# A 31-tap depthwise convolution: from POOL and diagonal matrices to 128x32 matrices over shifted copies

## The chip, the core and the metric

The kernel runs on one core of one Trainium2 chip. The metric is the device time of one execution in microseconds; the times are medians of several runs. Engines are named as the profile names them: PE (TensorE), DVE (VectorE), ACT (ScalarE), POOL (GpSimd) and SP (SyncE, which issues the DMAs).

## The reference, cut to what matters

The whole model is a chain of blocks over 256 positions of 1024 channels: attention with a chunked recurrent mixer, cross-attention, a feed-forward block, this convolution module, a sparse attention and more feed-forward blocks. The change lies in the convolution module alone:

```
def conformer_conv_module(h, w_in, b_in, w_dw, b_dw, ln_g, ln_b, w_out):
    a, g = jnp.split(h @ w_in + b_in, 2, axis=-1)
    u = a * jax.nn.sigmoid(g)
    u = lax.conv_general_dilated(
        u, w_dw[:, None, :].astype(u.dtype), window_strides=(1,),
        padding=[(CONV_WIDTH - 1, 0)], dimension_numbers=('NWC', 'WIO', 'NWC'),
        feature_group_count=D_MODEL) + b_dw
    uf = u.astype(jnp.float32)
    mu = jnp.mean(uf, axis=-1, keepdims=True)
    var = jnp.mean(jnp.square(uf - mu), axis=-1, keepdims=True)
    uf = (uf - mu) * lax.rsqrt(var + LN_EPS) * ln_g.astype(jnp.float32) + ln_b.astype(jnp.float32)
    u = jax.nn.silu(uf).astype(h.dtype)
    return u @ w_out
```

CONV_WIDTH is 31: each channel is convolved over time with its own 31 taps, causally. The input `h` is the normalised residual.

## The kernel before

Channels lie on the 128 partitions, in eight tiles (m = 0 to 7), time (256) along the free axis. For each tile `conformer` (L930) makes the two halves of the input product, the gated tile `cu`, the 31 taps, and its share of the sums for the layer norm; at the end all tiles are normalised and the output product (`proj("c_out")`, PE lines L215 to L217) follows.

The input product of tiles 0 to 2 is a split one (three fast passes, L215 to L217, 48 matmuls a tile), that of tiles 3 to 7 takes the weights as they were loaded, in fp32 (L990, 32 matmul rows, for tiles 3 and up). DVE multiplies it by the broadcast reciprocal root `bc_x` (L971, L973: `cag`), ACT applies tanh and bias (L975, L976), DVE forms `cu` (L977).

The taps of a tile are dealt out to three engines by two tables. PE takes CONV_PE taps (45 in all): ACT builds a diagonal matrix `cdg` for each (L1042) and PE multiplies `cu` by it into the bank `bt` (L1048). POOL takes CONV_GP taps (78): ACT makes the product `cpr` (L1028; the first of a tile L1025), POOL adds it to `cyp` (L1029). DVE takes the rest with fused multiply-adds on `cy` (L1011, L1013 the first, L1015 the others). DVE then adds the bank (L1057), POOL or DVE adds `cyp` (L1059), for tiles 0 to 2 a mean is subtracted (L1071, POOL), ACT squares (L338) and PE adds up the sums (L1077). Behind the last tile come mean, variance and root on DVE (L1091 and on), two broadcasts by PE (L327), the normalising on DVE and ACT and the split into `yy`. The residual is rescaled on DVE (L438), eight operations, by a second root `rs_g` that POOL computes (L303 to L312).

The order around the change is written out by hand: `CONF_AT` gives each step a due time and a spacing, and `timed()` steps generators by it; `need()` holds one until its input is there. A scheduler then orders the instructions per engine. SP issues only weight loads in this stretch: a raw tile is loaded (L181), ACT casts it (L198), DVE or POOL subtracts the cast (L200) for the split products.

Of the kernel before, what the change touches and what calls it, by code (L numbers as in the profile page):

```python
# [103 lines left out]
class Net:  # L104
# [825 lines left out]
    def conformer(self, first, pool):  # L930
        nc = self.nc
        W = 31
        us = [pool.tile([P, S], F32, name=f"cu{m}") for m in range(KT)]
# [3 lines left out]
        rb = zb = cb = None  # L937
        bt, yp = [None] * KT, [None] * KT
        have = set()

        def need(*keys):
            while not have.issuperset(keys):
                yield

        def tap(m, t):

            return wh[:, m * W + W - 1 - t : m * W + W - t]


        wh = pool.tile([P, KT * W], F32, name="cwh")  # L950
        o = POFF["c_w"][0]
        nc.gpsimd.tensor_scalar(wh, self.par[:, o : o + KT * W], 0.5, None, op0=ALU.mult)
        bh = pool.tile([P, KT], F32, name="cbh")
        o = POFF["c_bin"][0] + KT
        nc.gpsimd.tensor_scalar(bh, self.par[:, o : o + KT], 0.5, None, op0=ALU.mult)

        for m in range(KT):
            nc.vector.tensor_scalar(xg[:, m, :], self.x[:, m, :], gg[:, m : m + 1], None, op0=ALU.mult)

        def inp(m):  # L960
            nonlocal rb, zb
            b = b0
            if m:
                b, pb = product_of(m)
            yield
# [12 lines left out]
            have.add(f"u{m}")

        def product_of(m):  # L980
            nonlocal rb, zb
            w = self.chunk("c_in", m, **({"stop": "c_out"} if m < KT - 1 else {"room": 2}))
            pb = self.bank()
            b = [pb[:, 0:S], pb[:, S : 2 * S]]
            raw = [r.rearrange("p (k c) -> p k c", k=4) for r in w] if m >= CONV_N3 else None

            def product(i, k):
                c = slice(i * P, i * P + P)
                if raw:
                    nc.tensor.matmul(b[i][:, 0:S], raw[k // 4][:, k % 4, c], xg[:, k, :],  # L990
                                     start=(k == 0), stop=(k == KT - 1))
                else:
                    self.mm3(b[i][:, 0:S], w[k][:, :, c], self.xx[:, k], k == 0, k == KT - 1)

            for i in range(2):
                for k in range(KT):
                    product(i, k)
                if m == 1 and i == 0:
                    rb = self.bcast(r12, "x")
                    zb = self.zbank(2 * NT)  # L1000
            return b, pb
# [3 lines left out]
        def dv(m):  # L1005
            yield from need(f"u{m}")
            y, u = ys[m], us[m]
            if m > 2:
                yield from need("c")
                nc.scalar.activation(y, cb, AF.Identity, bias=self.col("c_b", m), scale=-1.0)  # L1010
                nc.vector.scalar_tensor_tensor(y, u, tap(m, 0), y, op0=ALU.mult, op1=ALU.add)  # L1011
            else:
                nc.vector.tensor_scalar(y, u, tap(m, 0), self.col("c_b", m), op0=ALU.mult, op1=ALU.add)  # L1013
            for t in range(1 + CONV_PE[m], W - CONV_GP[m]):
                nc.vector.scalar_tensor_tensor(y[:, t:S], u[:, 0 : S - t], tap(m, t), y[:, t:S], op0=ALU.mult, op1=ALU.add)  # L1015
                if t % 4 == 0:
                    yield
            have.add(f"d{m}")
            yield

        def gp(m):
            yield from need(f"u{m}")
            u, t0 = us[m], W - CONV_GP[m]
            y = yp[m] = pool.tile([P, S], F32, name="cyp", tag="cyp", bufs=4)
            nc.scalar.mul(y[:, t0:S], u[:, 0 : S - t0], tap(m, t0))  # L1025
            for t in range(t0 + 1, W):
                pr = pool.tile([P, S], F32, name="cpr", tag="cpr", bufs=4)
                nc.scalar.mul(pr[:, t:S], u[:, 0 : S - t], tap(m, t))  # L1028
                nc.gpsimd.tensor_tensor(y[:, t:S], y[:, t:S], pr[:, t:S], op=ALU.add)  # L1029
                if t % 4 == 0:  # L1030
                    yield
            have.add(f"g{m}")
            yield

        def pe(m):
            yield from need(f"u{m}")
            n = CONV_PE[m]
            for c in range(0, n, 4):
                dg = []
                for t in range(c + 1, min(c + 4, n) + 1):  # L1040
                    d = pool.tile([P, P], F32, name="cdg", tag="cdg", bufs=24)
                    nc.scalar.mul(d, self.ident, tap(m, t))  # L1042
                    dg.append(d)
                yield
                if c == 0:
                    bt[m] = self.bank("bt")
                for t, d in enumerate(dg, c + 1):
                    nc.tensor.matmul(bt[m][:, t:S], d, us[m][:, 0 : S - t], start=(t == 1), stop=(t == n))  # L1048
            have.add(f"p{m}")
            yield  # L1050

        def fin(m):
            nonlocal cb
            yield from need(f"d{m}", f"p{m}")
            y, t0 = ys[m], W - CONV_GP[m]
            if CONV_PE[m]:
                nc.vector.tensor_tensor(y[:, 1:S], bt[m][:, 1:S], y[:, 1:S], op=ALU.add)  # L1057
            yield from need(f"g{m}")
            (nc.gpsimd if m < KT - 2 else nc.vector).tensor_tensor(y[:, t0:S], yp[m][:, t0:S], y[:, t0:S], op=ALU.add)  # L1059
# [19 lines left out]
            have.add(f"s{m}")  # L1079
            yield  # L1080

        def rescale():
            yield from rest

        kinds = {"in": inp, "gp": gp, "dv": dv, "pe": pe, "fin": fin, "x": rescale}
# [556 lines left out]
```

## Time and profile before

| | us |
|---|---|
| median of three runs | 1132.01 (1129.48 to 1132.69) |
| the profiled execution | 1132.2 |
| span of its trace | 1130.4 |
| stage of the change in it: last residual sums to first output matmul | 440.5 to 566.2 |
| mean granted clock of PE over the span | 0.974 of full |

The profile is one execution. The table of stretches gives busy time per engine with the number of instructions and the clock granted to PE; the timeline gives in order of time the start, the length, the engine, the line and operation, the number of instructions run together in the row and, in brackets, the idle time of the engine ahead of it and what ended it. In both kernels the instructions of all other stages stand in the same order on each engine.

### The profile page before, as it was taken

The numbers are of one execution on the slowest core, as the hardware profiler recorded it, in microseconds if no ns is written. First come the engines' busy times: TensorE is split into PE (matmuls) and PEld (weight loads), VectorE is DVE, ScalarE is ACT, GpSimd is POOL, SyncE is SP. The second block draws the span as 40 slices with busy tenths as digits, with TensorE's granted clock in tenths as the row PEclk, the third lists the DMA queues.
The fourth block names the chain that finished last, engine by engine and source line by source line (L and its number), as shares of the span: only waits on it lengthen the run. The fifth ranks groups of instructions, "written<-read, shape, count | busy, mean of one in ns | idle before, by whom it ended". The sixth has DMA issues, their size and how long they took to land.

```text
span 1130.4 us, 19501 instructions
## 1 busy us (share of the span) xinstructions
PE 1070.3 (95%) x7282; PEld 984.6 (87%) x7282; DVE 827.4 (73%) x1654; ACT 638.2 (56%) x1231; POOL 195.4 (17%) x388
## 2 busy tenths in 40 slices
PE   6999999999999999697499999999999999999998
PEld 5899999999999889586398888889998898888887
DVE  5876667768888755999758777765568747777763
ACT  5675556556666544565366666544366746666531
POOL 5120003020000002677512000011332103000000
PEclk9999999999999999888599999999999999999999
DMA  7654444445555752222235565656235024555670
GB/s 233 220 167 158 127 147 155 128 135 191 187 193 178 219 169 71 65 85 93 75 113 176 190 191 183 223 173 189 95 112 189 18 76 149 188 190 192 179 208 31
DMA packets 52439, 171.38 MB, mean 152 GB/s; under 512 B 8440, under 2 KB 10360, under 8 KB 52344
## 3 DMA queue, kind: packets, MB, share of 16 engines
q1 hardware_dynamic: 52344, 170.14, 47.4%
q8 instruction: 57, 0.93, 0.3%
q14 instruction: 38, 0.31, 0.1%
HBM read 169.07 MB, written 1.05 MB: 150 GB/s over the span
## 4 chain that ended last, share of the span: by engine, by line
PE 79%; DVE 12%; ACT 3%; issue 2%; DMA 2%; POOL 1%; SPq 0%; POOLq 0%; ACTq 0%; DVEq 0%
PE pb L223 28%; PE pb L224 14%; PE pb L215 9%; PE pb L216 9%; PE pb L217 9%; DVE cy L1015 5%; DMA wraw<-in_w_in_dram 1%; ACT wpr L198 1%; DVE wpr L200 1%; DVE xx L278 1%; DVE xres L438 1%; DVE xres L395 1%; PE bh L1254 1%; DMA wraw<-in_n_out_dram 1%; PE zb L376 1%
## 5 line engine op out<-in xcount | busy, mean ns | idle before, releaser
L200 DVE TENSOR_TENSOR wpr<-wraw,wpr 128x1024 fp32r<-128x1024 f32 (+1 forms) x298 | 361.1, 1214 | 178.7 <-ACT wpr L198 176.4
L198 ACT CAST wpr<-wraw 128x1024 fp32r<-128x1024 f32 (+1 forms) x304 | 313.4, 1033 | 203.1 <-PE pb L224 96.0
L223 PE MATMUL pb<-xx,wpr 128*128 128x512 f32 x840 | 294.3, 393 | 0.0
L224 PE MATMUL pb<-xx,wpr 128*128 128x256 f32 x840 | 235.5, 280 | 0.0
L223 PEld LDWEIGHTS pb<-xx,wpr 128*128 128x128 f32 x840 | 158.5, 189 | 34.0
L223 PE MATMUL pb<-fhs,wpr 128*128 128x512 f32 x528 | 186.0, 394 | 0.0
L224 PEld LDWEIGHTS pb<-xx,wpr 128*128 128x128 f32 x840 | 158.5, 189 | 0.0
L224 PE MATMUL pb<-fhs,wpr 128*128 128x256 f32 x528 | 147.3, 279 | 0.0
L215 PE MATMUL pb<-xx,wpr 128*128 128x256 f32 x456 | 129.7, 287 | 7.7 <-ACT xx L277 7.7
L216 PE MATMUL pb<-xx,wpr 128*128 128x256 f32 x456 | 130.4, 287 | 2.5 <-DVE xx L278 2.5
L217 PE MATMUL pb<-xx,wpr 128*128 128x256 f32 x456 | 128.9, 283 | 0.0
L223 PEld LDWEIGHTS pb<-fhs,wpr 128*128 128x128 f32 x528 | 99.0, 187 | 23.0
L224 PEld LDWEIGHTS pb<-fhs,wpr 128*128 128x128 f32 x528 | 99.0, 188 | 0.0
L215 PEld LDWEIGHTS pb<-xx,wpr 128*128 128x128 f32 x456 | 86.7, 192 | 9.4 <-ACT xx L277 8.0
L216 PEld LDWEIGHTS pb<-xx,wpr 128*128 128x128 f32 x456 | 87.3, 191 | 4.2 <-DVE xx L278 3.3
L217 PEld LDWEIGHTS pb<-xx,wpr 128*128 128x128 f32 x456 | 87.4, 192 | 0.0
L215 PE MATMUL pb<-yy,wpr 128*128 128x256 f32 x256 | 73.1, 288 | 2.3 <-ACT yy L282 2.3
L216 PE MATMUL pb<-yy,wpr 128*128 128x256 f32 x256 | 72.7, 284 | 0.0
L217 PE MATMUL pb<-yy,wpr 128*128 128x256 f32 x256 | 72.6, 284 | 0.0
L1015 DVE SCALAR_TENSOR_TENSOR cy<-cu,cwh,cy 128x238 f32<-128x238 f32 (+18 forms) x117 | 71.6, 669 | 0.1
L869 ACT COPY ft<-pb 128x256 f32<-128x256 f32 x105 | 38.5, 368 | 55.2 <-PE pb L224 55.2
L1029 POOL TENSOR_TENSOR cyp<-cyp,cpr 128x229 f32<-128x229 f32 (+11 forms) x70 | 59.9, 860 | 26.1 <-ACT cpr L1028 22.0
(428 smaller groups left out, 2077.9 us busy)
## 6 DMA issues: line engine op xcount, KB each, us to landing
wraw<-in_up_dram SPq DMA_DIRECT2D x44, 512.0 KB, 4.0
wraw<-in_up2a_dram SPq DMA_DIRECT2D x44, 512.0 KB, 4.4
wraw<-in_up2b_dram SPq DMA_DIRECT2D x44, 512.0 KB, 3.8
wraw<-in_w_in_dram SPq DMA_DIRECT2D x22, 512.0 KB, 4.6
wraw<-in_n_in_dram SPq DMA_DIRECT2D x20, 512.0 KB, 4.1
wraw<-in_wkv_dram SPq DMA_DIRECT2D x16, 512.0 KB, 3.7
wraw<-in_dn_dram SPq DMA_DIRECT2D x16, 512.0 KB, 4.4
wraw<-in_c_in_dram SPq DMA_DIRECT2D x16, 512.0 KB, 4.1
```

Of the source, the lines that this page charges most:

```text
L198: self.nc.scalar.copy(hi, raws[j])
L200: lane.tensor_tensor(lo, raws[j], hi.bitcast(F32), op=ALU.subtract)
L215: mm(out, left[:, 0], right[:, 0], start=start, stop=False, skip_group_check=True)
L216: mm(out, left[:, 0], right[:, 1], start=False, stop=False, skip_group_check=True)
L217: mm(out, left[:, 1], right[:, 0], start=False, stop=stop, skip_group_check=True)
L223: mm(out, left[:, 0], right, start=start, stop=False, skip_group_check=True)
L224: mm(out[:, 0], left[:, 1], right[:, 0], start=False, stop=stop, skip_group_check=True)
L278: nc.vector.scalar_tensor_tensor(lo, src, g, hi.bitcast(F32), op0=ALU.mult, op1=ALU.subtract)
L376: self.nc.tensor.matmul(zb[:, tt : tt + 1], src[:, tt * P : tt * P + P], self.ones, start=(src is acc), stop=(src is sq))
L869: nc.scalar.copy(t, b[:, 1])
L1015: nc.vector.scalar_tensor_tensor(y[:, t:S], u[:, 0 : S - t], tap(m, t), y[:, t:S], op0=ALU.mult, op1=ALU.add)
L1029: nc.gpsimd.tensor_tensor(y[:, t:S], y[:, t:S], pr[:, t:S], op=ALU.add)
```

## The change

Nothing of the convolution runs on POOL any more, apart from clearing a margin, scaling a bias and the root `rs_g`. PE takes the first 4 x CONV_G[m] taps of tile m (12 for tiles 0 to 5, 16 and 24 for the last two), DVE the others (19, 15 and 7), 112 and 136 in all. The gated tiles now lie in one array `cuz` with 27 zeros ahead of each. `turn(m)` writes a tile to a DRAM buffer `cz` and reads it back into `crp` in another arrangement: partition 32j + c of block i holds channel 32i + c shifted by j, so one matrix of 128 rows and 32 columns sums four taps of 32 channels. Four such matmuls, one for each 32 channels, write four column ranges of 32 in the bank `bt` (a group); a tile has CONV_G groups. The matrices `cwd` come ready from DRAM (new input array `c_dw`, 1.8 MB, eight loads).

The due-time table is gone; a plain loop issues, for each m, the product and gate of tile m + 1, its turn, then the matmul taps, DVE taps and sums of tile m. The scaled input `cxg` is made by ACT instead of DVE, the means of tiles 0 to 2 are subtracted by DVE instead of POOL, and the second part of all output weights' conversion runs on DVE instead of POOL for six of the eight loads.

```diff
-CONV_PE = [4, 1, 1, 4, 1, 15, 11, 8]
-CONV_GP = [8, 10, 10, 10, 14, 6, 9, 11]
+CONV_G = [3, 3, 3, 3, 3, 3, 4, 6]
...
-        lane = self.nc.gpsimd if name == "c_out" and idx > 0 else self.nc.vector
-        lane.tensor_tensor(lo, raws[j], hi.bitcast(F32), op=ALU.subtract)
+        self.nc.vector.tensor_tensor(lo, raws[j], hi.bitcast(F32), op=ALU.subtract)
...
-        us = [pool.tile([P, S], F32, name=f"cu{m}") for m in range(KT)]
+        PAD = 4 * max(CONV_G) - 4
+        ZW = PAD + 3 + S
+        uz = pool.tile([P, KT, ZW], F32, name="cuz")
+        nc.gpsimd.memset(uz[:, :, 0 : PAD + 3], 0.0)
+        us = [uz[:, m, PAD + 3 :] for m in range(KT)]
+        dram = self.ctx.enter_context(self.tc.tile_pool(name="dram", bufs=1, space=bass.MemoryType.DRAM))
+        zs = [dram.tile([32, 4 * ZW], F32, name=f"cz{i}")[:, :] for i in range(4)]
...
+        wd = [pool.tile([P, n, P], F32, name=f"cwd{m}") for m, n in enumerate(CONV_G)]
+        for m, n in enumerate(CONV_G):
+            nc.sync.dma_start(wd[m], self.T["c_dw"][:, m, 0:n, :])
+        reps = [pool.tile([P, 4, ZW], F32, name=f"crp{i}") for i in range(3)]
...
+        def turn(m):
+            z = zs[m % 4]
+            nc.sync.dma_start(bass.AP(tensor=z.tensor, offset=0, ap=[[ZW, 4], [4 * ZW, 32], [1, ZW]]), uz[:, m, :])
+            nc.sync.dma_start(reps[m % 3].rearrange("p j x -> p (j x)")[:, 0 : 4 * ZW - 3],
+                              bass.AP(tensor=z.tensor, offset=0, ap=[[1, 4], [4 * ZW, 32], [1, 4 * ZW - 3]]))
+
+        def pe(m):
+            bt[m] = self.bank("bt")
+            n = CONV_G[m]
+            for i in range(n):
+                for j in range(4):
+                    c = slice(32 * j, 32 * j + 32)
+                    nc.tensor.matmul(bt[m][c, 0:S], wd[m][:, i, c], reps[m % 3][:, j, PAD - 4 * i : PAD - 4 * i + S],
+                                     start=(i == 0), stop=(i == n - 1))
...
-        timed([(u[0], u[1], kinds[u[2]](*u[3:])) for u in CONF_AT])
+        gated(0, None)
+        turn(0)
+        next(rest)
+        for m in range(KT):
+            if m + 1 < KT:
+                gated(m + 1, product(m + 1))
+                turn(m + 1)
+            if m == 0:
+                for k in range(KT):
+                    nc.scalar.mul(xg[:, k, :], self.x[:, k, :], gg[:, k : k + 1])
+            pe(m)
+            dv(m)
+            fin(m)
```

The order of the instructions at three places follows, first in the kernel before, then in the changed one; the lines of the changed kernel are lower by 14 ahead of the stage (L215 is L201 there, L327 is L313).

PE at the start of the stage, before: the broadcast of `rs_n` stands between matmuls of the product of tile 1 (`pb` from `wpr`), which has begun long before it.

```order
L216 MATMUL pb_5180<-xx_75,wpr_5043 128x256
L217 MATMUL pb_5180<-xx_75,wpr_5043 128x256
L215 MATMUL pb_5180<-xx_75,wpr_5043 128x256
L327 MATMUL bcb_5205<-ident_69,rs_n_5133 128x128 [waits DVE_49,PE_49]
L327 MATMUL bcb_5205<-ident_69,rs_n_5133 128x128
L216 MATMUL pb_5180<-xx_75,wpr_5043 128x256
L217 MATMUL pb_5180<-xx_75,wpr_5043 128x256
L215 MATMUL pb_5180<-xx_75,wpr_5043 128x256
L216 MATMUL pb_5180<-xx_75,wpr_5043 128x256
```

The same place after: both broadcasts, of `rs_n` and of POOL's `rs_g`, stand ahead of the product of tile 1.

```order
L202 MATMUL pb_4499<-xx_75,wfi_4571 128x256
L203 MATMUL pb_4499<-xx_75,wfi_4571 128x256
L313 MATMUL bcb_5189<-ident_69,rs_n_5133 128x128 [waits DVE_49,PE_49]
L313 MATMUL bcb_5189<-ident_69,rs_n_5133 128x128
L313 MATMUL bcb_5219<-ident_69,rs_g_5204 128x128 [waits PE_49,Pool_49]
L313 MATMUL bcb_5219<-ident_69,rs_g_5204 128x128
L201 MATMUL pb_5224<-xx_75,wpr_4976 128x256 [waits PE_49]
L202 MATMUL pb_5224<-xx_75,wpr_4976 128x256
L203 MATMUL pb_5224<-xx_75,wpr_4976 128x256
```

The broadcast of `rs_g`, which stood behind the input products of all tiles before, has moved ahead of that of tile 1.

SP, before: only loads of weights, each waiting for the matmuls or conversions that free its buffer.

```order
L181 DMA wraw_5534<-in_c_in_dram 128x1024 [waits DMAHW2_49,PE_49]
L181 DMA wraw_5536<-in_c_in_dram 128x1024 [waits DMAHW3_49,PE_49]
L181 DMA wraw_5561<-in_c_in_dram 128x1024 [waits DMAHW4_49,PE_49]
L181 DMA wraw_5563<-in_c_in_dram 128x1024 [waits DMAHW5_49,PE_49]
L181 DMA wraw_5725<-in_c_out_dram 128x1024 [waits DMAHW6_49,PE_49]
L181 DMA wraw_5727<-in_c_out_dram 128x1024 [waits DMAHW7_49,PE_49]
L181 DMA wraw_5732<-in_c_out_dram 128x1024 [waits DMAHW2_49,DVE_49]
```

SP after, from the turn of tile 3 (write `cz`, read `crp`) to the turn of tile 5; the read waits for the write of its own tile:

```order
L976 DMA cz3_5158<-cuz_5151 4x32x279 [waits DVE_49]
L977 DMA crp0_5184<-cz3_5158 128x1x1113 [waits DMAHW5_49,DMAHW4_49]
L168 DMA wraw_5570<-in_c_in_dram 128x1024 [waits PE_49]
L168 DMA wraw_5572<-in_c_in_dram 128x1024 [waits DMAHW7_49,PE_49]
L976 DMA cz0_5155<-cuz_5151 4x32x279 [waits DVE_49]
L977 DMA crp1_5185<-cz0_5155 128x1x1113 [waits DMAHW1_49,DMAHW0_49]
L168 DMA wraw_5638<-in_c_in_dram 128x1024 [waits DMAHW2_49,PE_49]
L168 DMA wraw_5640<-in_c_in_dram 128x1024 [waits DMAHW3_49,PE_49]
L976 DMA cz1_5156<-cuz_5151 4x32x279 [waits DVE_49]
L977 DMA crp2_5186<-cz1_5156 128x1x1113 [waits DMAHW5_49,DMAHW4_49]
```

Each pair of loads now stands behind a read that waits for a write, and each turn behind the loads of the pair ahead.

PE in the middle of the loop, before: products of two tiles follow each other, then the taps that stand ready.

```order
L990 MATMUL pb_5538<-cxg_5167,wraw_5480 128x256 x4
L990 MATMUL pb_5538<-cxg_5167,wraw_5482 128x256 x4
L990 MATMUL pb_5565<-cxg_5167,wraw_5534 128x256 [waits DMAHW6_49,PE_49]
L990 MATMUL pb_5565<-cxg_5167,wraw_5534 128x256 x3
L990 MATMUL pb_5565<-cxg_5167,wraw_5536 128x256 [waits DMAHW7_49]
L990 MATMUL pb_5565<-cxg_5167,wraw_5536 128x256 x3
L990 MATMUL pb_5565<-cxg_5167,wraw_5534 128x256 x4
L990 MATMUL pb_5565<-cxg_5167,wraw_5536 128x256 x4
L1048 MATMUL bt_5634<-cu3_5154,cdg_5604 128x255
L1048 MATMUL bt_5634<-cu3_5154,cdg_5606 128x254
L1048 MATMUL bt_5634<-cu3_5154,cdg_5608 128x253
```

PE after: the end of the product of tile 4 (`pb_5506`) with sums of tile 2 in it, the taps of tile 3 (`crp0`), the product of tile 5.

```order
L954 MATMUL pb_5506<-cxg_5167,wraw_5051 128x256
L1016 MATMUL zb_5194<-ones_71,sq_5496 128x1 [waits Activation_49]
L1016 MATMUL zb_5194<-ones_71,cy2_5161 128x1
L1016 MATMUL zb_5194<-ones_71,sq_5496 128x1
L954 MATMUL pb_5506<-cxg_5167,wraw_5056 128x256 x4
L986 MATMUL bt_5530<-crp0_5184,cwd3_5171 32x256 [waits DMAHW5_49,PE_49]
L986 MATMUL bt_5530<-crp0_5184,cwd3_5171 32x256 x11
L954 MATMUL pb_5574<-cxg_5167,wraw_5502 128x256 [waits DMAHW2_49,PE_49]
L954 MATMUL pb_5574<-cxg_5167,wraw_5502 128x256 x3
L954 MATMUL pb_5574<-cxg_5167,wraw_5504 128x256 [waits DMAHW3_49]
L954 MATMUL pb_5574<-cxg_5167,wraw_5504 128x256 x3
```

The product of tile m + 2 now always stands behind the matmul taps of tile m, which wait for a DMA.

## Rows read from the trace of the kernel before

**Rows 1.** PE's timeline. Columns: start us, length us, engine, line, operation, count, [idle <- releaser].

```profile
440.52 0.51 PE L415 MATMUL zb<-g,sq 128*128 128x2 f32 x4
...
481.64 0.74 PE L292 MATMUL zb<-ones,cy 128*128 128x1 f32 x4 [4.03 <-DVE zb L287]
...
483.65 16.49 PE L990 MATMUL pb<-cxg,wraw 128*128 128x256 f32 x64
...
499.98 2.30 PE L1048 MATMUL bt<-cu,cdg 128*128 128x255 f32 x10
...
503.82 7.15 PE L990 MATMUL pb<-cxg,wraw 128*128 128x256 f32 x32
...
556.06 0.59 PE L1077 MATMUL zb<-ones,cy 128*128 128x1 f32 x2 [2.52 <-DVE cy L1059]
...
566.16 0.58 PE L215 MATMUL pb<-yy,wpr 128*128 128x256 f32 x1 [2.34 <-ACT yy L282]
```

**Rows 2.** DVE's timeline, same columns.

```profile
441.06 0.16 DVE L320 TENSOR_SCALAR rv<-zb 128x2 f32<-128x2 f32 x1 [0.77 <-PE zb L415]
...
448.64 0.42 DVE L977 SCALAR_TENSOR_TENSOR cu<-cag 128x256 f32<-128x256 f32 x1 [0.34 <-ACT cag L975]
...
452.72 4.92 DVE L1015 SCALAR_TENSOR_TENSOR cy<-cu,cwh,cy 128x249 f32<-128x249 f32 x6
...
527.47 6.53 DVE L1015 SCALAR_TENSOR_TENSOR cy<-cu,cwh,cy 128x236 f32<-128x236 f32 x17
...
543.32 11.85 DVE L438 SCALAR_TENSOR_TENSOR xres<-xres,par,bc_x 128x256 f32<-128x256 f32 x8 [3.05 <-ACT bc_x L330]
...
555.60 0.40 DVE L1059 TENSOR_TENSOR cy<-cyp,cy 128x236 f32<-128x236 f32 x1
```

**Rows 3.** The page's head.

```profile
span 1130.4 us, 19501 instructions
```

**Rows 4.** Table of stretches; the first row names the columns.

```profile
core 0: us, PE busy (x) PEld busy (x) DVE busy (x) ACT busy (x) POOL busy (x), PEclk, DMA share, GB/s
...
441.00:453.00 12.00, 11.47 (x94) 11.25 (x94) 9.54 (x34) 9.29 (x28) 6.51 (x19) 1.00 0.00 0
...
474.00:532.00 58.00, 49.45 (x227) 42.85 (x225) 57.43 (x96) 32.46 (x79) 42.23 (x47) 0.89 0.31 100
...
532.00:556.00 24.00, 9.11 (x32) 8.14 (x32) 18.16 (x23) 9.90 (x20) 21.39 (x18) 0.57 0.25 77
...
441.00:566.00 125.00, 88.62 (x425) 77.88 (x424) 112.29 (x216) 67.99 (x167) 83.57 (x99) 0.80 0.22 72
```

**Rows 5.** Chain of waits through the stage, shares by line.

```profile
by line: DVE cy L1015 47.0%; issue 10.6%; DVE xres L438 8.0%; ACT cdg L1042 4.3%; DVE cu L977 3.1%; DVE cag L973 2.9%; ACT wpr L198 2.3%; DVE cy L1011 2.1%; ACT cpr L1028 2.0%; POOL cyp L1029 2.0%; PE bcb L327 2.0%; DVE cy L1098 1.7%; PE zb
```

**Rows 6.** Costliest groups: the page's for DVE, POOL's from 441 to 591 us.

```profile
L200 DVE TENSOR_TENSOR wpr<-wraw,wpr 128x1024 fp32r<-128x1024 f32 (+1 forms) x298 | 361.1, 1214 | 178.7 <-ACT wpr L198 176.4
...
L200 POOL TENSOR_TENSOR wpr<-wraw,wpr 128x1024 fp32r<-128x1024 f32 x6 | 14.8, 2471 | 18.3 <-ACT wpr L198 18.3
```

**Rows 7.** PE's timeline, two row tiles of 64, in a later stage.

```profile
817.94 0.70 PE L1352 MATMUL bs<-nkT,nqT 64*128 64x256 f32 x4
818.48 0.39 PE L1355 MATMUL bs<-nkT,nqT 64*128 64x128 f32 x4
```

**Rows 8.** DMA queue (packets, MB, share) and issues (count, KB each, us to landing).

```profile
q1 hardware_dynamic: 52344, 170.14, 47.4%
...
wraw<-in_wq_dram SPq DMA_DIRECT2D x8, 512.0 KB, 3.5
...
wraw<-in_dn2a_dram SPq DMA_DIRECT2D x8, 384.0 KB, 3.1
...
gw<-in_gate_w_dram SPq DMA_DIRECT2D x2, 16.0 KB, 5.0
```

**Rows 9.** POOL's timeline.

```profile
446.01 0.20 POOL L312 TENSOR_TENSOR rs_g<-rs_g,rt_g 128x2 f32<-128x2 f32 x1
```

**Rows 10.** Table of stretches, columns as in rows 4.

```profile
481.90:488.70 6.80, 6.55 (x19) 5.46 (x20) 6.24 (x11) 5.85 (x17) 6.29 (x9) 0.50 0.00 0
```

More of the change, by code (lines that the diff above doesn't have):

```diff
@@ L45 @@
     (4.681, 1, "v", 2), (4.986, 1, "v", 3), (5.392, 0.56, "out")]
-CONF_AT = [
[10 rows of a table removed]
-    (19.392, 0.476, "fin", 7)]
 NSA_AT = [
@@ L936, in conformer @@
         b0, (r12, rest, gg) = first
[L937 to L943, printed above, removed]
-        def tap(m, t):
[L947 to L965, printed above, removed]
+        bt, cb = [None] * KT, None
+        def tap(m, t):
+            return self.col("c_w", m * W + W - 1 - t)
@@ new lines, in conformer @@
+        wd = [pool.tile([P, n, P], F32, name=f"cwd{m}") for m, n in enumerate(CONV_G)]
+        for m, n in enumerate(CONV_G):
+            nc.sync.dma_start(wd[m], self.T["c_dw"][:, m, 0:n, :])
+        reps = [pool.tile([P, 4, ZW], F32, name=f"crp{i}") for i in range(3)]
+        bh = pool.tile([P, 2 * KT], F32, name="cbh")
+        o = POFF["c_bin"][0]
+        nc.gpsimd.tensor_scalar(bh, self.par[:, o : o + 2 * KT], 0.5, None, op0=ALU.mult)
+        rb = self.bcast(r12, "x")
+        zb = self.zbank(2 * NT)
@@ new lines, in product @@
+        def product(m):
+            w = self.chunk("c_in", m, **({"stop": "c_out"} if m < KT - 1 else {"room": 2}))
+            pb = self.bank()
+            raw = [r.rearrange("p (k c) -> p k c", k=4) for r in w] if m >= CONV_N3 else None
+            for i in range(2):
+                b, c = pb[:, i * S : i * S + S], slice(i * P, i * P + P)
+                for k in range(KT):
+                    if raw:
+                        nc.tensor.matmul(b, raw[k // 4][:, k % 4, c], xg[:, k, :], start=(k == 0), stop=(k == KT - 1))
+                    else:
+                        self.mm3(b, w[k][:, :, c], self.xx[:, k], k == 0, k == KT - 1)
+            return pb
@@ L966, in inp, with gated @@
+        def gated(m, pb):
             ag = pool.tile([P, 2, S], F32, name="cag", tag="cag", bufs=2)
             if m == 0:
-                while rb is None:
-                    yield
                 for i in range(2):
-                    nc.vector.tensor_tensor(ag[:, i, :], b[i][:, 0:S], rb, op=ALU.mult)
+                    nc.vector.tensor_tensor(ag[:, i, :], b0[i][:, 0:S], rb, op=ALU.mult)
             else:
@@ L977, in inp @@
             nc.vector.scalar_tensor_tensor(us[m], ag[:, 1, :], 1.0, ag[:, 0, :], op0=ALU.add, op1=ALU.mult)
[L978 to L1001, printed above, removed]
+        def turn(m):
[3 more added lines that the diff above has]
+                              bass.AP(tensor=z.tensor, offset=0, ap=[[1, 4], [4 * ZW, 32], [1, 4 * ZW - 3]]))
@@ L1005, in dv @@
+        def pe(m):
[6 more added lines that the diff above has]
+                                     start=(i == 0), stop=(i == n - 1))
         def dv(m):
-            yield from need(f"u{m}")
             y, u = ys[m], us[m]
+            t0 = 4 * CONV_G[m]
@@ L1008, in dv @@
             if m > 2:
-                yield from need("c")
                 nc.scalar.activation(y, cb, AF.Identity, bias=self.col("c_b", m), scale=-1.0)
-                nc.vector.scalar_tensor_tensor(y, u, tap(m, 0), y, op0=ALU.mult, op1=ALU.add)
             else:
-                nc.vector.tensor_scalar(y, u, tap(m, 0), self.col("c_b", m), op0=ALU.mult, op1=ALU.add)
-            for t in range(1 + CONV_PE[m], W - CONV_GP[m]):
+                nc.scalar.activation(y, u, AF.Identity, bias=self.col("c_b", m), scale=0.0)
@@ L1015, in dv @@
+            for t in range(t0, W):
                 nc.vector.scalar_tensor_tensor(y[:, t:S], u[:, 0 : S - t], tap(m, t), y[:, t:S], op0=ALU.mult, op1=ALU.add)
[L1016 to L1050, printed above, removed]
@@ L1052, in fin @@
         def fin(m):
             nonlocal cb
[L1054 to L1059, printed above, removed]
+            y = ys[m]
+            nc.vector.tensor_tensor(y, bt[m][:, 0:S], y, op=ALU.add)
@@ L1065, in fin @@
                 nc.vector.tensor_scalar(c0, z0[:, 0:NT], 1.0 / P, None, op0=ALU.mult)
-                yield
                 cb = self.bcast(c0, "mu", pool)
-                have.add("c")
             if m <= 2:
-                yield from need("c")
-                nc.gpsimd.tensor_tensor(y, y, cb, op=ALU.subtract)
-            yield
+                nc.vector.tensor_tensor(y, y, cb, op=ALU.subtract)
             sq = self.square(y)
-            yield
             for tt in range(NT):
@@ L1078, in fin @@
                                      start=False, stop=(m == KT - 1), skip_group_check=True)
[L1079 to L1085, printed above, removed]
-        timed([(u[0], u[1], kinds[u[2]](*u[3:])) for u in CONF_AT])
+        gated(0, None)
[6 more added lines that the diff above has]
+            if m == 0:
+                for k in range(KT):
+                    nc.scalar.mul(xg[:, k, :], self.x[:, k, :], gg[:, k : k + 1])
+            pe(m)
+            dv(m)
+            fin(m)
         zz = zb[:, 0 : 2 * NT].rearrange("p (t c) -> p t c", c=2)
@@ L1104, in conformer @@
         acc = self.proj("c_out")
+        next(rest)
         self.tap("x3")
@@ L1552, in layout @@
     A["c_out"] = _rb(I["conv_w_out_2"][0])
+    wd = np.zeros((32, D), np.float32)
+    wd[0:31] = I["conv_w_dw_2"][0][::-1]
+    dw = np.zeros((4, 32, KT, 8, 4, 32), np.float32)
+    wd = wd.reshape(8, 4, KT, 4, 32)
+    for c in range(32):
+        dw[:, c, :, :, :, c] = wd[:, :, :, :, c].transpose(1, 2, 0, 3)[::-1]
+    A["c_dw"] = dw.reshape(P, KT, 8, P)
     np_ = [h for a in (0, 8) for r in range(4) for h in (a + r, a + 4 + r)]
```

4 lines of the change are left out of this document (2 added, 2 removed), and 10 rows, old and new, of the table CONF_AT.

## The prediction

> **What bounds the kernel now.** The change touches one stage, the convolution module, so I first fixed where that stage lies. It begins where the last residual sums are read: PE's L415 row at 440.52 and DVE's first step on them at 441.06. It ends at the first matmul of the output product, PE's L215 row at 566.16 [rows 1, 2]. Work before and behind is written alike in both kernels, so the question is how far that 566.16 moves; the profiled execution took 1132.2 us with a span of 1130.4 [rows 3], and the median of the runs shown, 1132.0, is the same within 0.2, so the sum can be read against either.
>
> In the 125 us between, the table of stretches has DVE busy for 112.3, PE for 88.6 and POOL for 83.6, with PE's granted clock at 0.80; from 474 to 532 DVE is busy 57.4 of 58 [rows 4]. The chain of waits through the stage says the same by its longest pieces: 47% of it is DVE's tap line L1015, 8% is DVE's rescale L438 [rows 5]. So the DVE's taps bound the stage. They bound it at two prices: six taps took 4.92 us while POOL was adding its own (0.82 each), and seventeen took 6.53 (0.38 each) in a stretch where POOL stood in one operation; the eight rescales next to POOL's last additions took 11.85 [rows 2]. Behind the last tile there is a fixed tail: the last addition of tile 7 begins at 555.60 and the output product at 566.16, 10.6 us of sums, a mean, a reciprocal root, two broadcasts and normalising [rows 1, 2].
>
> **What goes.** POOL's 78 taps, their ACT products, PE's 45 diagonal taps and the table of due times go. With POOL silent I cost every DVE tap at 0.38. The 136 taps that remain are 52 us, with the other operations of a tile (0.6 gate, 0.33 product, 0.33 addition) 8.5 us for each of the first six tiles. Six of the eight subtractions of the output weights move to it from POOL, 1.21 each instead of POOL's 2.47 [rows 6], and seven now stand among the taps of tiles 5 to 7, 8.5 us. Up to the tail that is 52 + 12 + 3 (rescales) + 8.5 = 75.5 us of DVE, where 112.3 stand now with some 6 of the tail in it. So DVE ceases to bind, and the question is what binds next.
>
> **What comes: matmuls.** 112 fp32 matmuls of a 128x32 matrix replace 45 of 128x128. A tap of 255 columns takes 0.43 on PE (ten matmul rows, five taps, took 2.30, less the last one's drain) [rows 1]. If the four column tiles overlap fully, a tile of 12 is three such, 1.3 us; if they run one after another it is 12 x 0.43 = 5.2. No column tile stands in the trace. The nearest rows are two row tiles of 64: a matmul of 256 columns on each, and the next pair starts 0.54 after the first rather than 2 x 0.43 = 0.86 [rows 7]. That shows overlap in the array, though not full. I take 1.6 for a tile of three groups, and for tile 7 (six groups) 3.5, between 2.6 at full clock and 5.2 at half. [...]
>
> **What comes: the turn.** The four shifted copies are not made on an engine. SP writes a tile (128x279, 140 KB) to DRAM, waits, and reads it back as 128x1113 (557 KB). Such a pair is nowhere in the trace, so I bound it. A 512 KB load lands in 3.5 us and a 384 KB one in 3.1 [rows 8]: 128 KB are 0.4, so sixteen engines move 320 KB per us, 20 each, over a fixed 1.9. The queue's own row gives the same rate: 170.14 MB in 47.4% of 16 x 1130.4 us is 19.9 KB per us of a busy engine [rows 8]. Spread over sixteen engines a turn would be 1.9 + 0.4 + 1.9 + 1.7 = 6.0 us. But the DRAM side of both transfers is a pattern whose outermost dimension is 4, not 128. If only four engines carry it, the movement is four times as long: 1.9 + 1.7 + 1.9 + 7.0 = 12.5. The only transfer of before that isn't plain rows, the 16 KB gate weights, took 5.0, longer than 512 KB of plain rows [rows 8], so shape does set the time; I take 12.5 and keep 6.0 as the other end. To it comes queueing: a 512 KB load ahead on the same engine is 32 KB, 1.6 us, and I put half of that in, T = 13.3. [...]
>
> **The sum.** Start: in the new order on PE both broadcasts stand ahead of the product of tile 1, and the second waits for POOL's root, whose last step begins at 446.01 [rows 9]. So PE idles some 5 us that were filled before, and product 1 ends near 453.3. The gated tile 0 is ready at 449, as before (448.64 plus 0.42) [rows 2], since two rescales ahead of it cost what the wait for ACT did. Its 19 taps, beside tile 1's eleven and eight rescales, last until about 465 (38 x 0.39); the sums and the broadcast of tile 0 take 2.5 more, and the split product 2 (48 matmuls at 0.12, as 94 took 11.47 from 441 to 453 [rows 4], and part of it at half clock) ends near 473.7. Product 3 then follows tile 1's taps, 473.7 + 1.6 + 7.2 = 482.5.
>
> Loop: on PE the order is product m+1, taps of m, product m+2. A raw product of 32 matmuls takes 7.15 [rows 1] and the sums 0.9. PE needs 9.7 per tile and DVE 8.5. But product m+2 stands behind the taps of m, which wait for the turn of m, which waits for product m: two tiles cost 2.2 (gate, ACT, product) + T + 1.6 + 8.1 = 25.2, or 12.6 a tile. PE then idles about 3 us a tile, and the trace shows what that does: behind an idle of 4.03 the granted clock was 0.50 from 481.9 to 488.7, and 64 raw matmuls took 16.49 instead of 14.3 [rows 1, 10]. I add 1 us per product: 26.2 for two tiles. From product 3 to product 7 are two such pairs: 482.5 + 52.4 = 534.9.
>
> End: gate and product of tile 7 take 2.9, to 537.8. Its turn takes 13.3 and about 3.5 of waiting on SP, where the loads of the output weights, each waiting for a buffer, stand between turn 6 and turn 7: 554.6. Taps 3.5, addition 0.6, and the tail of 10.2 behind it: the output product starts at 568.9, 2.7 later than now. **1132.2 + 2.7 = 1135**. Each microsecond of T counts three times (two pairs and the last turn), so T = 12.4 would be no change, T = 11.5 gives 1130 and T = 15 gives 1140.
>
> **Rivals.** *Sixteen engines.* With T = 6.0 two tiles of the loop cost 17.9, less than PE's 2 x 9.7, so PE binds: product 7 at 482.5 + 4 x 9.7 = 521.3, gated tile at 524.2. Its copies would be there by 532, but DVE still has 17 taps, four subtractions and two additions, 12.1 us, to 536.3; 10.2 behind it the output starts at 546.5, 19.7 earlier: **1112.5**, faster. For it: every load of rows seen runs on all engines. Against: the outermost 4, and the gate weights' row. The border is T = 12.4.
>
> *Column tiles one after another.* A tile's taps take 5.2: product 3 slips 3.6, two pairs 7.2, and tile 7's 24 matmuls take 10.3 at full clock instead of 3.5, with part at half 12. 568.9 + 3.6 + 7.2 + 8.5 = 588: **1154**, slower. Against it stand the row tiles' rows [rows 7]. Half overlap (2.6 a tile, 5.2 for the last) gives 1.0 + 2.0 + 1.7 to 3: **1140**.
>
> *It does not relieve DVE.* If a tap took 0.6, between the 0.38 and 0.82 of rows 2, 136 would take 82 us, DVE's work 105, and from 449 it would end at 554: **1131**, no change. The seventeen taps at 0.38 speak against it, since nothing else is seen to slow them but POOL.
>
> **Chances.** Four engines with overlapping tiles 0.55 (1128 to 1142: faster 0.06, same 0.27, slower 0.22); sixteen engines 0.20 (faster nearly always, 0.18); tiles one after another 0.13; half overlap 0.12. A difference under 0.3%, 3.4 us, can't be told from none. Faster 0.24, same 0.30, slower 0.46. The range reaches into both outer cases and leaves out their far halves: 1112 to 1152; the likeliest case's own is 1128 to 1142.
>
> **What the changed profile would show.** Reads of the copies landing 8.5 to 10 us behind their issue, writes 3 to 4 (four engines) or under 4 and 2.5 (sixteen). PE's idle time ahead of its tap line ended by that DMA, about 3 us a tile. A tile's twelve matmuls in 1.3 to 2 us. DVE taps at 0.38 to 0.4 with a DVE idle of several us a tile. Product 7 near 535, the last taps near 555. I am wrong if DVE has no idle time in the loop, if the twelve take 5 us, or if the turn is hidden because products are as slow as it.

## The result and the profile after

The changed kernel takes 1163.6 us in the median (1161.2 to 1166.5), before 1132.3: 1.028 times as long, with a 95% interval of 1.025 to 1.032. The forecast was 1135 with a range of 1112 to 1152, so the time lies 29 us above where it was expected and 12 above the top of the range. The direction that held most of the chance, slower, was right; the size was not.

In the profiled execution of the changed kernel (1165.4 us, span 1163.6; before 1130.4 [rows 3]) the stage ends at 598.65, where it ended at 566.16 before [rows 1]. The table of stretches over the whole stage and over the loop in it (columns as in rows 4):

```profile
core 0: us, PE busy (x) PEld busy (x) DVE busy (x) ACT busy (x) POOL busy (x), PEclk, DMA share, GB/s
441.00:598.00 157.00, 91.83 (x569) 68.94 (x568) 85.56 (x217) 27.06 (x54) 2.36 (x13) 0.75 0.42 105
474.00:555.00 81.00, 55.04 (x332) 42.00 (x330) 42.55 (x98) 9.74 (x18) 0.00 (x0) 0.83 0.43 104
```

DVE is busy for 85.6 us of 157, where it was busy for 112.3 of 125 [rows 4]; POOL has gone from 83.6 to 2.4. No engine is close to full any more, so the stage is bound by something that is no engine. The chain of waits through the stage, shares by line, names it (before: [rows 5]):

```profile
by line: DMA crp<-cz 32.0%; DMA cz<-cuz 19.1%; PE pb L954 14.3%; PE bt L986 9.6%; DVE cy L998 3.1%; PE zb L1016 3.1%; issue 2.0%; PE pb L203 1.8%; PE pb L201 1.7%; PE bcb L313 1.6%; PE pb L202 1.5%; DVE cy L1043 1.3%; DVE cuz L969 0.9%; DVE
```

Half of it is the turn: 32% the read of the copies, 19% the write. DVE's tap line, 47% before, is at 3%. The timeline of PE, matmul taps and the first output matmul (columns as in rows 1), shows where the idle time stands:

```profile
460.73 2.79 PE L986 MATMUL bt<-crp,cwd 128*32 128x256 f32 x24 [9.10 <-DMA crp<-cz]
...
476.21 1.50 PE L986 MATMUL bt<-crp,cwd 128*32 128x256 f32 x24
...
511.65 2.79 PE L986 MATMUL bt<-crp,cwd 128*32 128x256 f32 x24 [6.16 <-DMA crp<-cz]
...
528.25 2.79 PE L986 MATMUL bt<-crp,cwd 128*32 128x256 f32 x24 [5.64 <-DMA crp<-cz]
...
544.83 2.79 PE L986 MATMUL bt<-crp,cwd 128*32 128x256 f32 x24 [5.39 <-DMA crp<-cz]
547.55 7.82 PE L954 MATMUL pb<-cxg,wraw 128*128 128x256 f32 x32
...
582.91 4.05 PE L986 MATMUL bt<-crp,cwd 128*32 128x256 f32 x34 [14.01 <-DMA crp<-cz]
...
598.65 1.22 PE L201 MATMUL pb<-yy,wpr 128*128 128x256 f32 x4 [2.34 <-ACT yy L268]
```

The taps of tiles 3, 4 and 5 start 16.6 us apart, each behind 5.4 to 6.2 us of idle time that the read of the copies ended. A group of 24 matmul rows (12 matmuls, one tile) takes 1.50 in the row where PE comes from work, 2.79 in those where it comes from a wait; the granted clock was 1.00 in the one (476.21 to 477.71) and 0.50 in the others (511.65 to 514.44, for one). The queue of SP for the same stretch (start, length of the issues, count):

```profile
447.51 0.61 SPq L976 DMA_DIRECT2D cz<-cuz  x1
451.21 0.57 SPq L977 DMA_DIRECT2D crp<-cz  x1
...
488.15 0.54 SPq L976 DMA_DIRECT2D cz<-cuz  x1
498.44 0.53 SPq L977 DMA_DIRECT2D crp<-cz  x1
...
507.95 0.55 SPq L976 DMA_DIRECT2D cz<-cuz  x1
515.55 0.53 SPq L977 DMA_DIRECT2D crp<-cz  x1
520.02 2.95 SPq L168 DMA_DIRECT2D wraw<-in_c_in_dram  x2
525.06 0.56 SPq L976 DMA_DIRECT2D cz<-cuz  x1
532.17 0.53 SPq L977 DMA_DIRECT2D crp<-cz  x1
...
558.30 0.54 SPq L976 DMA_DIRECT2D cz<-cuz  x1
...
567.33 0.54 SPq L977 DMA_DIRECT2D crp<-cz  x1
```

Read against PE's rows, the first turn takes 447.51 to 460.73, 13.2 us: 3.7 until the write has landed and the read is issued, 9.5 for the read. The turn of tile 4 takes 507.95 to 528.25, 20.3: 7.6 and 12.7. Its write was issued while the read of tile 3, issued at 498.44, was still under way; that read ended at 511.65 on PE, and the write landed 3.9 later. The turns of tiles 3 and 5 take 23.5 (488.15 to 511.65) and 19.8 (525.06 to 544.83), the last one 24.6 (558.30 to 582.91).

### The profile page after: what moved, and what is told of

Read it like the earlier page. It is cut to its first block, busy times and chain, and to the rows that moved or that the text cites. A ratio compares the mean times of both kernels' runs of the same rounds, so it can differ in the third digit from the quotient of the medians.

```text
span 1163.6 us, 19574 instructions
## 1 busy us (share of the span) xinstructions
PE 1073.4 (92%) x7416; PEld 974.9 (84%) x7416; DVE 803.4 (69%) x1664; ACT 597.8 (51%) x1119; POOL 113.3 (10%) x303
## 4 chain that ended last, share of the span: by engine, by line
PE 79%; DMA 9%; DVE 6%; ACT 2%; POOL 2%; issue 2%; SPq 0%; ACTq 0%; POOLq 0%; DVEq 0%
PE pb L209 26%; PE pb L210 13%; PE pb L201 9%; PE pb L202 9%; PE pb L203 9%; DMA crp<-cz 4%; DMA cz<-cuz 3%; PE pb L954 2%; PE bt L986 1%; DVE wpr L186 1%; DVE xx L264 1%; ACT wpr L185 1%; DMA wraw<-in_n_in_dram 1%; DVE xres L381 1%; DMA wraw<-in_w_in_dram 1%
## 5 line engine op out<-in xcount | busy, mean ns | idle before, releaser
L186 DVE TENSOR_TENSOR wpr<-wraw,wpr 128x1024 fp32r<-128x1024 f32 (+1 forms) x304 | 367.2, 1210 | 183.5 <-ACT wpr L185 181.2
L201 PE MATMUL pb<-xx,wpr 128*128 128x256 f32 x456 | 131.5, 291 | 7.5 <-ACT xx L263 7.5
L201 PEld LDWEIGHTS pb<-xx,wpr 128*128 128x128 f32 x456 | 88.2, 195 | 9.2 <-ACT xx L263 7.8
L986 PE MATMUL bt<-crp,cwd 128*32 128x256 f32 x224 | 25.7, 589 | 56.0 <-DMA crp<-cz 47.2
L201 PE MATMUL pb<-yy,wpr 128*128 128x256 f32 x256 | 73.2, 288 | 2.3 <-ACT yy L268 2.3
L986 PEld LDWEIGHTS bt<-crp,cwd 128*32 128x32 f32 x224 | 9.9, 153 | 66.0 <-issue 65.5
```

The costliest lines, as they stand in the source:

```text
L186: self.nc.vector.tensor_tensor(lo, raws[j], hi.bitcast(F32), op=ALU.subtract)
L201: mm(out, left[:, 0], right[:, 0], start=start, stop=False, skip_group_check=True)
L986: nc.tensor.matmul(bt[m][c, 0:S], wd[m][:, i, c], reps[m % 3][:, j, PAD - 4 * i : PAD - 4 * i + S], start=(i == 0), stop=(i == n - 1))
```

## The experiments

The theory (A) with which I went on: both transfers of a turn run on four DMA engines, as forecast, and these four carry everything else that falls into the same time too, so a turn costs far more in the loop than alone. The rivals: (B) the way through DRAM and SP's wait for the write cost the time, whatever the number of engines; (C) the half clock behind each wait stretches the loop.

**Weight loads out of the loop.** Products 3 to 7 take one block of weights that is loaded ahead of the stage.

```diff
-            w = self.chunk("c_in", m, **({"stop": "c_out"} if m < KT - 1 else {"room": 2}))
+            if m < CONV_N3:
+                w = self.chunk("c_in", m, stop="c_out")
+            else:
+                if m == KT - 1:
+                    self.run_ahead(room=2)
+                w = [wc, wc]
```

> The changed kernel with the turns as they are, but without weight loads in the loop: the products of tiles 3 to 7 all take one block of weights loaded ahead of the stage (the weights of the other products are left out), so the output weights' loads move ahead of the turns as well. Theory A: every turn takes the 13.3 us that the first one took with nothing beside it; two tiles cost 2.2 + 13.3 + 2.8 + 8.7 = 27 instead of 34, and the last turn 13 instead of 24.6, in all some 25 us less than the changed kernel: 1136 to 1143. Rival C (the loop is slow because PE's clock is at half behind each wait, and the turns are long in any case): within 6 us of the changed kernel's 1163.

Measured: 1151.6 us, ratio to before 1.018 (1.016 to 1.020), 12 us less than the changed kernel and 9 more than the top of the forecast. The queue of SP and the taps on PE in the second half of the loop:

```profile
515.76 0.53 SPq L983 DMA_DIRECT2D cz<-cuz  x1
519.46 0.53 SPq L984 DMA_DIRECT2D crp<-cz  x1
```

```profile
528.73 2.79 PE L993 MATMUL bt<-crp,cwd 128*32 128x256 f32 x24 [4.98 <-DMA crp<-cz]
540.03 1.50 PE L993 MATMUL bt<-crp,cwd 128*32 128x256 f32 x24
556.45 3.64 PE L993 MATMUL bt<-crp,cwd 128*32 128x256 f32 x32 [6.92 <-DMA crp<-cz]
```

With no load beside it, that turn takes 515.76 to 528.73, 13.0 us, as the first one of the changed kernel did, and two tiles take 27.7 (528.73 to 556.45; forecast 27) instead of 33.2. So the loads cost the loop some 5.5 us for two tiles. Part of the expected gain wasn't there because the loads had only moved: the turns of tiles 0, 2 and 3, now beside them, took 16 to 19 us. The clock (C) is not the main part: taps behind a wait still take 2.79 (3.64 for tile 6, with sixteen matmuls), the granted clock over the whole run is 0.961, in the changed kernel 0.962, and yet the time has fallen by more than C allowed.

**All engines for the turn, eight DMAs.** Each transfer is cut in four of 32 rows.

```diff
-            nc.sync.dma_start(bass.AP(tensor=z.tensor, offset=0, ap=[[ZW, 4], [4 * ZW, 32], [1, ZW]]), uz[:, m, :])
...
+            for i in range(4):
+                nc.sync.dma_start(bass.AP(tensor=z.tensor, offset=i * ZW, ap=[[4 * ZW, 32], [1, ZW]]),
+                                  uz[32 * i : 32 * i + 32, m, :])
+            for j in range(4):
+                nc.sync.dma_start(flat[32 * j : 32 * j + 32, 0 : 4 * ZW - 3],
+                                  bass.AP(tensor=z.tensor, offset=j, ap=[[4 * ZW, 32], [1, 4 * ZW - 3]]))
```

> The changed kernel with each turn cut into eight DMAs of 32 rows (four writes, four reads), so that the outermost dimension of every pattern is 32 instead of 4; the same bytes, the same packets, the same DRAM buffer. Theory A (four DMA engines carry a turn, and share themselves with the weight loads): a turn falls from 20 us in the loop to 7 to 9 (two fixed times of 1.9, six more issues at 0.35, 2.2 us of movement), PE binds the loop at about 9.7 a tile, the output product starts near 550: 1115 to 1125. Rival B (the round trip through DRAM and SP's wait for the write cost the time, not the number of engines): the turn stays at 13 or more and the time between 1150 and 1165.

Measured: 1145.8 us (1139.8 to 1151.9), ratio 1.012 (1.008 to 1.017): 18 less than the changed kernel, but outside both forecasts. The first turns did what A says: that of tile 0 took 7.5 us, that of tile 2 7.6; the last two, among loads of the output weights, took 10.7 and 11.9. Most of the time went elsewhere. What PE waited for in the stage (total us, times, longest):

```profile
PE zb L1020 <- DVE cy L1007: 15.3, 5, 6.6
PE zb L278 <- DVE cy L1007: 10.4, 1, 10.4
PE bt L990 <- DMA crp<-cz: 9.0, 4, 5.0
```

Its waits for the copies fell from 47 us, in six, to 9. But with eight DMAs a turn the scheduler had put PE's and DVE's instructions in another order: the sums of a tile stand ahead of most of a product on PE and wait 15.3 us for DVE's additions, while DVE waits 19.9 for such products. DVE's taps also became dearer. In both kernels, where a tap follows one of the same tile it starts 0.50 us behind it, and where taps of two tiles alternate 0.37 (medians of the trace's records); of the neighbouring pairs of taps 37 of 107 are of the first kind in the changed kernel, 87 of 111 here. How the loss divides between these is not shown. So this run changes two things and can't decide between A and B alone.

**The read's pattern, two dimensions swapped.** This is the one that can: on every engine the instructions and their order are those of the changed kernel.

```diff
-                              bass.AP(tensor=z.tensor, offset=0, ap=[[1, 4], [4 * ZW, 32], [1, 4 * ZW - 3]]))
+                              bass.AP(tensor=z.tensor, offset=0, ap=[[4 * ZW, 32], [1, 4], [1, 4 * ZW - 3]]))
...
-    A["c_dw"] = dw.reshape(P, KT, 8, P)
+    A["c_dw"] = np.ascontiguousarray(dw.transpose(1, 0, 2, 3, 4, 5)).reshape(P, KT, 8, P)
```

> The changed kernel with the first two dimensions of the read's pattern swapped, [1 x 4, 1116 x 32, 1 x 1113] to [1116 x 32, 1 x 4, 1 x 1113], and the rows of the matrices permuted to match: the same two DMAs a turn, the same packets of 4452 bytes, and on every engine the same instructions in the same order. The write keeps its outermost 4. Theory A: the read leaves the four engines, lasts 1.9 + 1.8 instead of 9 to 15, a turn takes 7.5 to 9; two tiles of the loop cost 2.2 + 8.5 + 1.5 + 8.1 = 20.3 against PE's 18.9, so 10.2 a tile, and the last turn loses some 14: the output product near 553, 1118 to 1126. Rival B (the round trip itself): no change, 1158 to 1168.

Measured: 1120.1 us (1119.0 to 1121.2), ratio 0.990 (0.988 to 0.991), within the forecast of A: 43 us less than the changed kernel by the order of two dimensions. The write, still on an outermost 4, takes 3.7; the read now takes 3.8 (452.63 on SP to 456.47 on PE) instead of 9.5:

```profile
448.94 0.61 SPq L976 DMA_DIRECT2D cz<-cuz  x1
452.63 0.58 SPq L977 DMA_DIRECT2D crp<-cz  x1
```

```profile
456.47 1.50 PE L986 MATMUL bt<-crp,cwd 128*32 128x256 f32 x24 [3.60 <-DMA crp<-cz]
...
497.67 1.50 PE L986 MATMUL bt<-crp,cwd 128*32 128x256 f32 x24 [1.17 <-DMA crp<-cz]
507.10 1.50 PE L986 MATMUL bt<-crp,cwd 128*32 128x256 f32 x24
517.29 1.50 PE L986 MATMUL bt<-crp,cwd 128*32 128x256 f32 x24 [0.69 <-DMA crp<-cz]
```

These tiles, 3 to 5, are 9.4 and 10.2 us apart and wait 1.2 us at most. B falls: the way through DRAM and the wait for the write are all still there. That four engines carry a narrow transfer, and not a slow pattern all of them, shows in the table of stretches, first of the changed kernel while only the read of tile 0 and the write of tile 1 are under way, both with an outermost 4, then of this one while only the read of tile 0 is:

```profile
457.00:460.50 3.50, 0.00 (x0) 0.00 (x0) 3.50 (x11) 0.00 (x0) 0.00 (x0) 0.50 0.25 85
```

```profile
453.50:455.30 1.80, 0.00 (x0) 0.00 (x0) 1.73 (x6) 0.91 (x2) 0.00 (x0) 1.00 0.71 230
```

The DMA share is 0.25, four of sixteen, at 85 GB/s, against 0.71, eleven of sixteen on the mean, at 230. Per busy engine that is 21 GB/s and 20, so the engines work no faster with the new pattern; there are more of them. The trace's records of single packets agree: while the read of tile 0 moved its 128 packets of 4452 bytes, 3.9 were under way at a time in the changed kernel (452.57 to 459.87) and 12.7 in this one (453.97 to 456.05).

**The products one tile further ahead.** The changed kernel with product m + 2 emitted ahead of the taps of m; the turns stay on four engines.

```diff
-            if m + 1 < KT:
-                gated(m + 1, product(m + 1))
-                turn(m + 1)
+            if m + 2 < KT:
+                gated(m + 2, product(m + 2))
+                turn(m + 2)
```

> The changed kernel, its turns as they are on four engines, with the products one tile further ahead as in the kernel with the direct turn. Theory A in the form that the wait is dear because product m + 2 stands behind the taps of m: now product m + 3 does, three tiles share one turn, 2.2 + 20 + 2 + 8.5 = 33 for three instead of 34 for two, 11 to 12 a tile as far as the four engines can carry it (their share of a tile's two transfers and two loads is 1.7 + 7.0 + 3.2 = 11.9): the output product 16 to 22 earlier, 1141 to 1150. If the four engines are already full in the changed kernel's loop, the time stays at 1158 to 1166.

Measured: 1155.7 us, ratio 1.022 (1.020 to 1.023), 8 less than the changed kernel and between the two forecasts, 6 above the first and 2 below the second. On SP the write now follows its neighbour's read at once, and the reads are still 15.7 to 16.4 us apart:

```profile
492.50 0.53 SPq L977 DMA_DIRECT2D crp<-cz  x1
493.09 0.94 SPq L168 DMA_DIRECT2D wraw<-in_c_in_dram  x2
494.08 0.66 SPq L976 DMA_DIRECT2D cz<-cuz  x1
508.19 0.54 SPq L977 DMA_DIRECT2D crp<-cz  x1
...
523.96 0.54 SPq L977 DMA_DIRECT2D crp<-cz  x1
```

The write issued at 494.08 has landed only at 508.19, 14.1 us later, behind the read and the loads issued ahead of it. A tile's share of the four engines was to be 1.7 (write) + 7.0 (read) + 3.2 (two loads) = 11.9, well under that. The packet records show what fills the time: packets of the read, the loads and the write follow each other without a gap from 493.86 to 507.66, 13.8 us, and then none with data moves for 1.9, until the next read, which had to wait for the write, begins. That makes the 15.7 measured. So turns of neighbouring tiles did not overlap here, although the products stood further ahead; that no other order would get below 15.7 a tile is not shown. This is the half of theory A that I had not stated.

**Turn without DRAM.** Four DMAs read the gated tile directly, each row four times, shifted by one.

```diff
+            for i in range(4):
+                a = uz[32 * i : 32 * i + 32, m, 0 : ZW - 3]
+                nc.sync.dma_start(reps[m % 3][:, i, 0 : ZW - 3],
+                                  bass.AP(tensor=a.tensor, offset=a.offset, ap=[a.ap[0], [1, 4], [1, ZW - 3]]))
```

> The changed kernel with the turn made without DRAM: four DMAs read the gated tile's 32 channels of a block four times, each shifted by one, straight into the 128 partitions of the copies (channel c shifted by j on partition 4c + j; the matrices' rows are permuted to match). Outermost dimensions 32 and 128, 512 packets of 1104 bytes. Theory A: a turn takes 1.3 us of issues, one fixed time of 1.9 and about 2 of movement, some 5 us; PE binds the loop at 9.7 a tile and the output product starts at 545 to 550: 1111 to 1118. Rival B predicts the same gain here as theory A, but none in the kernel with eight DMAs through DRAM; if small packets or reads of the on-chip memory are slow, the turn is over 10 us and the time 1125 or more.

Measured: 1115.5 us (1112.1 to 1117.0), ratio 0.985 (0.983 to 0.988), as forecast. The taps of tiles 2 to 5 on PE are 9.43 us apart, with no wait, and the table of stretches has PE busy throughout and at full clock:

```profile
487.18 1.50 PE L984 MATMUL bt<-crp,cwd 128*32 128x256 f32 x24
...
496.61 1.50 PE L984 MATMUL bt<-crp,cwd 128*32 128x256 f32 x24
...
547.46 1.23 PE L201 MATMUL pb<-yy,wpr 128*128 128x256 f32 x4 [2.34 <-ACT yy L268]
```

```profile
477.00:524.00 47.00, 47.00 (x319) 37.48 (x318) 41.53 (x97) 8.58 (x17) 0.00 (x0) 1.00 0.60 161
```

**Taps from one turn.** All tiles' matmuls read tile 0's copies.

```diff
-                turn(m + 1)
...
-                    nc.tensor.matmul(bt[m][c, 0:S], wd[m][:, i, c], reps[m % 3][:, j, PAD - 4 * i : PAD - 4 * i + S],
+                    nc.tensor.matmul(bt[m][c, 0:S], wd[m][:, i, c], reps[0][:, j, PAD - 4 * i : PAD - 4 * i + S],
```

> The changed kernel with the turn of tile 0 alone: the matmul taps of all tiles read tile 0's copies (the turns of tiles 1 to 7 are left out), so no product waits for a DMA. It shows what is left without the turns. Theory A: PE's 9.7 a tile or DVE's taps bind, 1110 to 1116. If column tiles or the half clock cost much by themselves, 1125 or more.

Measured: 1113.0 us (two timed runs, 1112.3 and 1113.7), ratio 0.983 (0.981 to 0.986). Without seven of the eight turns the kernel is 51 us faster than the changed one and 2.5 from the kernel with the direct turn. So the turns cost these 51 us, and the direct one hides nearly all of its own.

**Direct turn and products further ahead.** The direct turn as above, and with it the loop that makes the products one tile earlier; this one is meant as a kernel to keep.

```diff
+            if m + 2 < KT:
+                gated(m + 2, product(m + 2))
+                turn(m + 2)
+            pe(m)
```

> The kernel with the direct turn (four DMAs, no DRAM) and in addition the products one tile further ahead: product m + 2 stands ahead of the matmul taps of tile m, so product 2 no longer waits behind the sums of tile 0. In the direct kernel PE stood still for 10.1 us ahead of those sums; if that idle time lies on the path, 5 to 9 us are won: 1107 to 1111. If DVE's taps of tiles 0 and 1 are what the start waits for, the idle time only moves: 1113 to 1117, no change.

Measured: 1107.9 us in the median (1105.3 to 1117.2), ratio 0.981 (0.976 to 0.985), 7.6 less than the direct turn alone by the medians, which is what was forecast for idle time on the path. That it lay on the path is not shown. The two ranges overlap, since one of its four runs took 1117, and the trace is of that run. In it the idle time ahead of tile 0's sums has halved, yet the output product starts later than the 547.46 of the direct kernel, whose trace is of its fastest run; first the direct kernel's row, then this one's:

```profile
465.74 1.01 PE L278 MATMUL zb<-ones,cy 128*128 128x1 f32 x4 [10.13 <-DVE cy L1001]
```

```profile
466.79 0.98 PE L278 MATMUL zb<-ones,cy 128*128 128x1 f32 x4 [5.28 <-DVE cy L1001]
...
549.27 1.22 PE L201 MATMUL pb<-yy,wpr 128*128 128x256 f32 x4 [2.34 <-ACT yy L268]
```

It is faster than the kernel before by the whole interval, and faster than the direct kernel only by the medians.

## Why the prediction was wrong, step by step

*What bounds the kernel now, and what goes*: right in that the stage no longer waits for DVE once POOL's part is gone. DVE stands idle for 18.3 us ahead of the last addition. The price of a tap was right only in part: fifteen take 5.62 us (0.375 each; forecast 0.38) where two tiles alternate, as in the seventeen that the forecast went by [rows 2], but 0.50 each where one tile's taps follow each other, 0.42 on the mean. The 136 taps come to 56.5 us instead of 52. The fifteen, and the idle time:

```profile
558.19 5.62 DVE L998 SCALAR_TENSOR_TENSOR cy<-cuz,par,cy 128x235 f32<-128x235 f32 x15
...
589.23 0.42 DVE L1003 TENSOR_TENSOR cy<-bt,cy 128x256 f32<-128x256 f32 x1 [18.28 <-PE bt L986]
```

*Column tiles*: right. A tile of twelve takes 1.50 at a granted clock of 1.00 (forecast 1.6), where twelve matmuls of 0.43 one after another would take 5.2: on the mean 3.4 of the four column tiles work at once. The rivals of tiles one after another and of half overlap (2.6) fall.

*The turn, alone*: right. 13.2 us against 12.5 before queueing; four engines, as taken. No row of before shows four engines for an outermost 4: the four in T were my assumption. The changed kernel shows a DMA share of 0.25, four of sixteen, while only transfers with an outermost 4 were under way (457.00 to 460.50). The rival of sixteen, given 0.20, did not happen.

*The loop*: this is the step that failed. The prediction put "half of that in, T = 13.3" for a load ahead on the same engines, and then let two tiles share "2.2 (gate, ACT, product) + T + 1.6 + 8.1". Two things were mis-sized in this term. Each turn in the loop meets a whole pair of loads: the read of tile 4 took 12.7, which is the 9.5 of the first one and the pair's 3.2. And both turns of a pair of tiles need the same four engines, so the write of a tile also waits for the read of its neighbour: 7.6 instead of 3.7. T was 19.8 to 23.5 (20.3 in the turn of tile 4), not 13.3, and two tiles took 33.2 (511.65 to 544.83), not 26.2. On the path of the two pairs stood the turns of tiles 3 and 5, 16.7 us more than twice 13.3. The numbers for it were in the prediction: 1.7 + 7.0 a turn and 1.6 a load, which for two tiles are 23.8 us on each of four engines, and 31.4 with four fixed times of 1.9 in full (an estimate; the kernel with the products further ahead shows 15.7 a tile). I counted the chain of one tile and never the load on the resource.

*The difference, term by term* (forecast 568.9 for the output product, found 598.65):

| term | forecast | found | difference |
|---|---|---|---|
| end of product 3 | 482.5 | 485.7 | +3.2 |
| products 3 to 7, two pairs of tiles | 52.4 | 69.7 | +17.3 |
| last turn with its wait on SP | 16.8 | 24.6 | +7.8 |
| taps of tile 7 | 3.5 | 6.3 | +2.8 |
| last addition and tail | 10.8 | 9.4 | -1.4 |

(Product 7 ends at 547.55 + 7.82 = 555.4; the gate and product of tile 7 took the forecast 2.9.) The last turn failed in the same way as the loop: its write was issued before the read of tile 6 had landed, and loads of the output and next weights stood around it. The taps of tile 7 began at half clock (granted 0.50 from 582.91 to 585.30; 2.79 for 24 rows would be 3.95 for the 34, measured 4.05) and had the sums of tile 6 among them; their own rows come to 5.3 us, where the forecast's upper end was 5.2.

*The clock*: I added 1 us per product. In the changed kernel the loop ran at 0.83 of full, in the direct kernel at 1.00. A product behind taps at half clock took 7.82 (granted clock 0.91) instead of 7.15 (1.00, before), within that 1 us; the taps' 2.79 instead of 1.50 came on top, 1.3 a tile. Beside the 6.5 to 10 us that each turn on the path took too long this is the small part.

*The rivals*: of the one of sixteen engines the arithmetic is borne out by the kernels with a wide turn: it had PE bound at 9.7 a tile and the output product at 546.5, 1112.5; the direct kernel has 9.43 a tile and 547.46, 1115.5. Its border, a turn of 12.4, means little: with four engines full it is not one turn's time that counts but all that they carry.

*The range*: its top, 1152, was set by the rival of serial column tiles, and the likeliest case's own, 1142, by a T a little above 15. The four engines' load of 31.4 for a pair of tiles, instead of 26.2, would have put the likeliest case 10 us higher, at 1145, and its upper end at 1152 (estimates from the same rows). That is still 12 below the 1163.6 measured.

## What to carry to other kernels

When a transfer's pattern confines it to a few DMA engines, don't price it alone: add up what all transfers of a loop turn put on those engines, with the time that a read waits for its write, and compare that sum with the loop's period. Before building a loop around such a transfer, try its dimensions in another order: here the swap of two dimensions was worth 43 us at the same bytes, and a kernel that lost 3% became one that gains 1%. And compare the order of the instructions whenever a variant has another number of them; the variant with eight DMAs would have spoken against a right theory.

## What the runs showed that I had not expected

A transfer on four engines moved 85 GB/s (a DMA share of 0.25), and the same read in the other order 230 GB/s at a share of 0.71, in the same kernel apart from two dimensions. A read of the on-chip copy of a tile in 512 pieces of 1104 bytes, shifted by one element each, is not slow: the last direct turn, four issues with weight loads around, took 5.5 us until PE could start (527.73 to 533.21), where the way through DRAM with the wide read took 7.5 for the first (448.94 to 456.47) and 10.1 for the last (528.82 to 538.95). And with POOL silent a DVE tap cost 0.37 where two tiles alternate and 0.50 where one tile's taps follow each other, against the 0.82 beside POOL [rows 2].
